# Order of VectorE's steps in the dense expert stage: subtractions behind gather steps, the steps halved and issued in quarters

## The chip, the cores and the metric

The kernel runs on one core of a Trainium2 chip. The metric is the device time of one execution in microseconds. The median of three runs of the kernel before is 2719.4 us (2717.3 to 2721.43).

## What is computed

Two transformer blocks over 512 tokens of width 1024. The change lies in the expert layer of the first, which picks 16 of 16384 experts per head and token:

```python
def peer_ffn(h, w_pq, sub_keys, expert_u, expert_v):
    ...
        q = (hb @ w_pq).reshape(TOK_BLOCK, PEER_HEADS, 2, PEER_DHALF)
        s = jnp.einsum('thpd,hpnd->thpn', q, sub_keys).astype(jnp.float32)
        ...
        top_s, pos = lax.top_k(cand_s, PEER_TOPK)
        idx = jnp.take_along_axis(cand_i, pos, axis=-1)
        gate = jax.nn.softmax(top_s, axis=-1).astype(hb.dtype)
        u = expert_u[idx]
        act = jax.nn.gelu(jnp.einsum('thkd,td->thk', u, hb), approximate=False)
        vv = expert_v[idx]
        return jnp.einsum('thk,thkd->td', gate * act, vv)
```

## The kernel before, in words

The expert layer treats the first 384 tokens and the last 128 differently. For the 384 it goes **densely** over all 16384 experts in 128 blocks of 128: up (the block's rows of `expert_u` times the tokens), gelu, times a gate that is zero where an expert was not chosen, and down (times the rows of `expert_v`), summed over all blocks in six banks. For the last 128 tokens it **gathers** the chosen rows with indirect DMAs that GpSimd issues. The dense loop is `peer_dense`, the gather `peer_gather`; a third strand, `ada`, computes the second block's modulation on VectorE. They run at the same time: `peer_dense` yields a weight, and the loop in `peer` that called it then takes as many steps of the other two as the weight is worth. All is written out when the kernel is built, so that this loop only sets the order in which each engine finds its instructions. Each engine takes them in that order.

Products are made of three matmuls with operands split in a high and a low half. ScalarE copies the high half (`whi`, `wh`, `uh`), and VectorE subtracts it from the source for the low half (`wlo`, `wl`, `ul`). In iteration i of the dense loop:

- `weigh(i - 1)` multiplies the activation with its gate on VectorE (`ga`, L1379), copies `wh` on ScalarE and returns the subtraction for `wl` (L1382) as something to be called later;
- `act(i)` is the gelu of block i out of its bank (ScalarE, L1371);
- `trans(i + 2, q)` transposes one half of a block of `expert_u` on TensorE (L1354, four transposes into the one bank `pt`), copies `uh` out of the bank and subtracts `ul` out of it (both in `split`, L86 and L87). The bank is free for the next transposes when `ul` has been read;
- `values(i - 1)` splits the rows of `expert_v` into `whi` and `wlo` (L86, L87);
- `down(i - 2, ...)` and `up(i + 1)` are the matmuls (L67 to L69), 18 with 512 columns and 24 with 384.

On TensorE an iteration is: transposes q = 0, down, transposes q = 1, up. The low halves follow their high halves at once on VectorE, but for `wl`, which is called after `trans(i + 2, 0)`. The loop yields twice per iteration, behind the first three pairs of `down` and at the end.

28 of the 128 blocks are **early**: their up and gelu were done in an earlier stage (`peer_early`), and the dense loop only loads the result. They come in groups of four between the others; an iteration of one has half the weight and neither transposes nor up.

A step of `peer_gather` for index i issues the fetch of a row of `expert_u` (`ur`) and one of `expert_v` (`vr`), two steps ahead of their use; multiplies row i of `ur` with the token's activations (L1763, the product); and adds a weighted row of `vr` to the output (L1770, the accumulation). Row buffers are four deep. A piece of the next head's selection (L1578 to L1665, a chain of short VectorE instructions) comes ahead of the product in about half of the steps. A step of `ada` is one multiply-add (L1853) on a loaded tile `aw`. There are 154 units of gather steps and 56 of `ada` steps, taken 2% ahead of the dense loop's share.

Of the kernel before, what the change touches and what calls it, by code (L numbers as in the profile page):

```python
# [10 lines left out]
F32 = mybir.dt.float32  # L11
F32R = mybir.dt.float32r
# [4 lines left out]
AF = mybir.ActivationFunctionType  # L17
ALU = mybir.AluOpType
# [4 lines left out]
D = 1024  # L23
NB = S // 128
KD = D // 128
# [30 lines left out]
class Kern:  # L56
# [1084 lines left out]
    def peer(self):  # L1141
        tc, nc, A, xt, ah, al = self.tc, self.nc, self.A, self.xt, self.ah, self.al
        v, s, pe, g = nc.vector, nc.scalar, nc.tensor, nc.gpsimd
        self.ad = self.es.enter_context(self.pool("ada"))
        self.banks = self.es.enter_context(self.pool("banks", space=PSUM))
        with self.pool("peer") as pp, self.pool("gdram", space=bass.MemoryType.DRAM) as dp:
            self.gd = dp.tile([ND // ST, NKEYS, NKEYS, ST], F32, name="gd")
            self.vb = A["expert_v"][0].rearrange("(n e) d -> n e d", e=128)
            self.ad_d = dp.tile([EARLY, 128, ND], F32, name="early")
            hT = pp.tile([128, D], F32, name="hT")  # L1150
            sc3 = pp.tile([128, 2 * HEADS, NKEYS], F32, name="sc3")
            self.lim = pp.tile([128, 2, TOPK, TOPK], F16, name="lim")
            self.num = pp.tile([128, TOPK], F16, name="num")
            for a in range(TOPK):
                for i, x in enumerate((self.START[a], a)):
                    g.memset(self.lim[:, i, a, :], float(x))
                g.memset(self.num[:, a:a + 1], float(self.CAND[a]))
            with self.pool("ptmp", side="right") as tmp:
                sel = [tmp.tile([128, NB - 1, HEADS, TOPK], F32, name=f"sel{i}") for i in range(3)]
                with self.pool("pkeys", side="right") as kp:  # L1160
                    KT = kp.tile([128, 16, 128], F32, name="KT")
                    with self.pool("pnrm", side="right") as t2:
                        self.attn_out(t2, Banks(self.banks, lin=range(4), tr=(4, 5)), hT, KT)
                    ps = Banks(self.banks, lin=(6, 7, 0, 1), sc=(2, 3), gp=(2, 3, 6, 7), eu=(4, 5))
                    self.early = self.peer_early(tmp, ps)
                    with self.pool("psel", side="right") as t2:
                        self.peer_select(t2, ps, sel, sc3, KT)
                with self.pool("pspr", side="right") as t2:
                    self.peer_spread(t2, ps, sel)
                for _ in self.early:  # L1170
                    pass
            with self.pool("pgat") as gp:
                ps = Banks(self.banks, pt=(4,), pu=(5,), **{f"pv{b}{i}": ((6, 7, 0, 1, 2, 3)[2 * b + i],) for b in range(3) for i in range(2)})
                gath = self.peer_gather(gp, NB - 1, hT, sc3)
                side = self.ada(self.ad, gp, ps)
                dense = self.peer_dense(gp, ps, itertools.chain(gath, side), hT)
                load, done = 0.0, [0, 0]
                for w in dense:
                    load += w
                    for i, (it, n) in enumerate(((gath, HEADS * TOPK + TOPK + 10), (side, 6 * (KD + 1) + 2))):  # L1180
                        while done[i] < load * n * self.HASTE:
                            next(it, None)
                            done[i] += 1
        self.show("x2", xt)
# [120 lines left out]
    def peer_dense(self, dp, ps, others, hT):  # L1305
# [35 lines left out]
                    gates[i + j] = gt[:, :, j, :]  # L1341

        def trans(i, q):
            if i >= NE or order[i] < EARLY:
                return
            if i < FIRST:
                return
            if q == 0:
                ut[i] = [dp.tile([128, KD, 128], F32R, name=nm, bufs=2) for nm in ("uh", "ul")]
            u = us[i][:, q * 512:q * 512 + 512]  # L1350
            if order[i] >= self.nt:
                p = ps.tile([128, 512], F32, name="pt")
                for j in range(4):
                    pe.transpose(p[:, j * 128:j * 128 + 128], u[:, j * 128:j * 128 + 128], self.ident)  # L1354
                u = p
            h, l = (t[:, 4 * q:4 * q + 4, :].rearrange("p k e -> p (k e)") for t in ut[i])
            self.split(h, l, u)

        def up(i):
            if i >= NE or order[i] < EARLY:  # L1360
# [22 lines left out]

        def values(i):
            if not 0 <= i < NE:
                return
            vs[i] = [self.ring.tile([128, D], F32R, name=nm, bufs=self.SPL) for nm in ("whi", "wlo")]
            self.split(*vs[i], raw.pop(i))

        def down(i, parts):  # L1390
            if i < 0:
# [14 lines left out]
        for i in range(NE):  # L1406
            load(i + 3)
            load2(i + 1)
            low = weigh(i - 1)
            act(i)  # L1410
            trans(i + 2, 0)
            low()
            values(i - 1)
            down(i - 2, pairs[:3])
            w = (0.5 if i + 1 < NE and order[i + 1] < EARLY else 1.1) / (1.1 * NE - 0.6 * EARLY)
            yield w / 2
            down(i - 2, pairs[3:])
            trans(i + 2, 1)
            up(i + 1)
            ws.pop(i - 2, None), vs.pop(i - 2, None)  # L1420
            yield w / 2
        for _ in others:
            pass
        weigh(NE - 1)()
        values(NE - 1)

        items = self.it_glu[0]
        own = [it for item in items for it, _, _ in item]
# [283 lines left out]
    def peer_gather(self, gp, b, hT, sc3):  # L1712

        nc, A, xt = self.nc, self.A, self.xt
        v, s, g = nc.vector, nc.scalar, nc.gpsimd
        U, V = A["expert_u"][0], A["expert_v"][0]
        idx, gates = {}, {}

        def select(h):
            sv, si = ([gp.tile([128, 1, TOPK], dt, name=f"{n}{c}", bufs=2) for c in range(2)]  # L1720
                      for n, dt in (("sv", F32), ("si", U32)))
            for c in range(2):
                self.top16(gp, sc3[:, 2 * h + c:2 * h + c + 1, :], sv[c], si[c])
                yield
            out = [gp.tile([128, 1, TOPK], F32, name=f"sel{i}", bufs=3) for i in range(3)]
            yield from self.pairs(gp, sv, si, out, v)
            yield
            yield from self.softmax16(gp, out[2])
            idx[h] = gp.tile([128, TOPK], I32, name="idx", bufs=3)
            v.scalar_tensor_tensor(idx[h], out[0][:, 0, :], float(NKEYS), out[1][:, 0, :], op0=ALU.mult, op1=ALU.add)  # L1730
            gates[h] = out[2][:, 0, :]
            yield

        def rows(tab, h, k, name):
            t = gp.tile([128, D], F32, name=name, bufs=4)
            g.indirect_dma_start(out=t, out_offset=None, in_=tab,  # L1736
                                 in_offset=bass.IndirectOffsetOnAxis(ap=idx[h][:, k:k + 1], axis=0))
            return t


        AHEAD, n = 2, HEADS * TOPK
        acts, ur, vr = {}, {}, {}
        sel = select(0)
        for i in range(-AHEAD, n + TOPK):
            j = i + AHEAD
            if j < n:
                if j % TOPK == 0:
                    for _ in sel:
                        if j == 0:
                            yield  # L1750
                    sel = select(j // TOPK + 1) if j + TOPK < n else iter(())
                else:
                    next(sel, None)
                ur[j] = rows(U, j // TOPK, j % TOPK, "ur")
            if TOPK <= j < n + TOPK:
                j -= TOPK
                vr[j] = rows(V, j // TOPK, j % TOPK, "vr")
            if 0 <= i < n:
                h, k = divmod(i, TOPK)
                if k == 0:  # L1760
                    acts[h] = gp.tile([128, TOPK], F32, name="act", bufs=2)
                u = ur.pop(i)
                v.scalar_tensor_tensor(u, u, 1.0, hT, op0=ALU.mult, op1=ALU.mult, accum_out=acts[h][:, k:k + 1])  # L1763
            if i >= TOPK:
                h, k = divmod(i - TOPK, TOPK)
                act = acts[h]
                if k == 0:
                    s.activation(act, act, AF.Gelu)
                    v.tensor_tensor(act, act, gates[h], op=ALU.mult)
                v.scalar_tensor_tensor(xt[:, b, :], vr.pop(i - TOPK), act[:, k:k + 1], xt[:, b, :], op0=ALU.mult, op1=ALU.add)  # L1770
            yield
# [500 lines left out]
```

## Time and profile before

| | |
|---|---|
| median of the runs | 2719.4 us |
| profiled execution | 2718.3 us, span 2716.5 us |
| busy TensorE / VectorE / ScalarE / GpSimd | 2482.5 / 1843.2 / 1009.9 / 820.2 us |
| mean granted clock of TensorE | 0.967 |
| dense stage | about 917 to 2026 us |
| 128 gate products `ga` (L1379) | 907.6 to 2016.5 us (starts) |
| 128 row products (L1763) | 982.9 to 1898.4 us (starts) |

TensorE is PE in the profile, VectorE DVE, ScalarE ACT, GpSimd POOL, SyncE SP. An idle time is put to the engine and line that ended it: "PE bank L1354 <- DVE ul L87" is TensorE, about to transpose at L1354, waiting for the `ul` subtraction. L1354 is the transposes, L67 to L69 the matmuls of both `up` and `down`. A matmul's listed duration overlaps the next one's; its pace is the distance of the starts.

### The profile page before, as it was taken

To read this page: it belongs to the slowest core of one execution; us is meant where nothing else is said; L and a number is where in the kernel's file an instruction comes from. 1 tells how busy PE (TensorE), PEld (TensorE's weight loads), DVE (VectorE), ACT (ScalarE), POOL (GpSimd) and SP (SyncE) were. 2 spreads that over 40 slices of the span, in tenths; PEclk is the share of its full clock that TensorE was granted. 3 is DMA by queue.
4 is the path that set the end of the run, shared out by engine and by line. 5 is a ranking of instruction groups with operands and counts; after the bars stand their busy time and mean duration, and the time that the engine had idled before them with its cause. 6 is when DMAs were issued, how large, how long until landed. Compare 5 with 4: busy or idle time off the path is not lost. (4 is left out here: it accounts for less than half of the span.)

```text
span 2716.5 us, 39721 instructions
## 1 busy us (share of the span) xinstructions
PE 2482.5 (91%) x15452; PEld 2076.9 (76%) x15452; DVE 1843.2 (68%) x3701; ACT 1009.9 (37%) x1589; POOL 820.2 (30%) x759
## 2 busy tenths in 40 slices
PE   7999996899788799999998999999999889899998
PEld 6775774687677789788787888889877667788887
DVE  4725654569899475877877787878666856644546
ACT  4424443433288333233232333333343224444321
POOL 3324200224500011333333333333114715433322
PEclk9999998899899899999999999999999989899999
DMA  4111246431256567888888888888742214133232
GB/s 144 43 40 55 87 170 215 159 110 62 68 224 259 207 240 258 290 295 292 297 285 284 308 296 293 308 314 301 250 136 62 78 39 142 48 96 95 93 109 77
DMA packets 222004, 484.28 MB, mean 178 GB/s; under 512 B 15560, under 2 KB 129881, under 8 KB 220280
## 3 DMA queue, kind: packets, MB, share of 16 engines
q1 hardware_dynamic: 184248, 347.29, 37.7%
q0 software_dynamic: 37568, 134.46, 13.9%
q8 instruction: 121, 1.98, 0.3%
q14 instruction: 67, 0.55, 0.1%
HBM read 432.67 MB, written 49.02 MB: 177 GB/s over the span
## 5 line engine op out<-in xcount | busy, mean ns | idle before, releaser
L1736 POOL DMA_INDIRECT ur<-in_expert_u,idx x128 | 199.3, 1557 | 776.4 <-DVE ur L1763 517.8
L86 ACT ACTIVATE whi<-raw 128x1024 fp32r<-128x1024 f32 (+1 forms) x266 | 278.4, 1047 | 410.5 <-PE bank L68 234.8
L87 DVE TENSOR_TENSOR wlo<-raw,whi 128x1024 fp32r<-128x1024 f32 (+1 forms) x199 | 250.8, 1260 | 171.0 <-ACT whi L86 167.2
L87 POOL TENSOR_TENSOR wlo<-raw,whi 128x1024 fp32r<-128x1024 f32 (+1 forms) x67 | 176.1, 2628 | 562.8 <-ACT whi L86 540.8
L67 PE MATMUL bank<-whi,wh 128*128 128x512 f32 x768 | 313.5, 408 | 2.6 <-ACT whi L86 2.5
L68 PE MATMUL bank<-wlo,wh 128*128 128x512 f32 x768 | 306.3, 399 | 2.8 <-DVE wlo L87 2.8
L69 PE MATMUL bank<-whi,wl 128*128 128x512 f32 x768 | 306.3, 399 | 0.0
L69 PE MATMUL bank<-ah,wlo 128*128 128x512 f32 (+2 forms) x688 | 272.4, 396 | 14.6 <-POOL wlo L87 10.8
L67 PE MATMUL bank<-ah,uh 128*128 128x384 f32 (+1 forms) x816 | 281.7, 345 | 2.5 <-ACT ga L1371 2.5
L67 PE MATMUL bank<-ah,whi 128*128 128x512 f32 (+2 forms) x688 | 274.4, 399 | 1.5 <-ACT ah L1527 0.9
L68 PE MATMUL bank<-al,uh 128*128 128x384 f32 (+1 forms) x816 | 273.6, 335 | 1.4 <-POOL al L1822 1.3
L69 PE MATMUL bank<-ah,ul 128*128 128x384 f32 (+1 forms) x816 | 273.2, 335 | 0.0
L68 PE MATMUL bank<-al,whi 128*128 128x512 f32 (+2 forms) x688 | 272.0, 395 | 0.0
L87 DVE TENSOR_TENSOR ul<-bank,uh 128x512 fp32r<-128x512 f32 x194 | 133.8, 690 | 201.8 <-ACT uh L86 201.8
L1381 ACT ACTIVATE wh<-ga 128x384 fp32r<-128x384 f32 x128 | 67.2, 525 | 532.6 <-DVE ga L1379 491.9
L86 ACT ACTIVATE uh<-bank 128x512 fp32r<-128x512 f32 x194 | 115.2, 594 | 171.2 <-PE bank L1354 171.2
L1736 POOL DMA_INDIRECT vr<-in_expert_v,idx x128 | 136.7, 1068 | 125.3 <-DVE xt L1770 91.1
L68 PEld LDWEIGHTS bank<-wlo,wh 128*128 128x128 f32 x768 | 145.9, 190 | 35.8 <-DVE wlo L87 4.7
L67 PEld LDWEIGHTS bank<-whi,wh 128*128 128x128 f32 x768 | 146.0, 190 | 34.2 <-ACT whi L86 3.7
L69 PEld LDWEIGHTS bank<-whi,wl 128*128 128x128 f32 x768 | 145.5, 189 | 34.5
L1354 PE MATMUL bank<-ident,ub 128*128 128x128 f32 x776 | 120.8, 279 | 55.7 <-DVE ul L87 45.2
L69 PEld LDWEIGHTS bank<-ah,wlo 128*128 128x128 f32 x688 | 132.1, 192 | 47.1 <-POOL wlo L87 13.0
(585 smaller groups left out, 5673.6 us busy)
## 6 DMA issues: line engine op xcount, KB each, us to landing
raw<-in_expert_v SPq DMA_DIRECT2D x128, 512.0 KB, 5.2
ub<-in_expert_u SPq DMA_DIRECT2D x97, 512.0 KB, 4.4
raw<-in_w_in SPq DMA_DIRECT2D x48, 512.0 KB, 3.8
gd<-gst SPq DMA_DIRECT2D x12, 2048.0 KB, 7.1
gb<-gd SPq DMA_DIRECT2D x32, 768.0 KB, 8.0
aw<-in_w_ada SPq DMA_DIRECT2D x48, 512.0 KB, 7.9
raw<-in_w_up SPq DMA_DIRECT2D x44, 512.0 KB, 3.6
utd<-wlo SPq DMA_DIRECT2D x31, 512.0 KB, 3.0
```

The costliest lines, as they stand in the source:

```text
L67: mm(ps, lh, rh, start=first, stop=False)
L68: mm(ps, lh, rl, start=False, stop=False)
L69: mm(ps, ll, rh, start=False, stop=last)
L86: self.nc.scalar.activation(hi, src, AF.Copy)
L87: (eng or self.nc.vector).tensor_tensor(lo, src, hi.bitcast(F32), op=ALU.subtract)
L1354: pe.transpose(p[:, j * 128:j * 128 + 128], u[:, j * 128:j * 128 + 128], self.ident)
L1381: s.activation(wh, a, AF.Copy)
L1736: g.indirect_dma_start(out=t, out_offset=None, in_=tab, in_offset=bass.IndirectOffsetOnAxis(ap=idx[h][:, k:k + 1], axis=0))
```

## The change

The subtractions of `trans` and `values` are no longer issued with their high halves. Both functions now return them, as `weigh` did, and the loop calls them behind a yield. It yields four times per iteration, a quarter of the weight each. A gather step is divided in two by a yield between the product and the accumulation, and its number of units goes from 154 to 300. In an iteration VectorE so gets: `ga`; first portion of the other strands; `wl`, `ul` of q = 0; second portion; `wlo`; third portion; `ul` of q = 1; fourth portion.

```diff
-                    for i, (it, n) in enumerate(((gath, HEADS * TOPK + TOPK + 10), (side, 6 * (KD + 1) + 2))):
+                    for i, (it, n) in enumerate(((gath, 2 * (HEADS * TOPK + TOPK) + 12), (side, 6 * (KD + 1) + 2))):
...
         def trans(i, q):
-            if i >= NE or order[i] < EARLY:
-                return
-            if i < FIRST:
-                return
+            if i >= NE or order[i] < EARLY or i < FIRST:
+                return lambda: None
...
-            self.split(h, l, u)
+            s.activation(h, u, AF.Copy)
+            return lambda: v.tensor_tensor(l, u, h.bitcast(F32), op=ALU.subtract)
...
         def values(i):
             if not 0 <= i < NE:
-                return
-            vs[i] = [self.ring.tile([128, D], F32R, name=nm, bufs=self.SPL) for nm in ("whi", "wlo")]
-            self.split(*vs[i], raw.pop(i))
+                return lambda: None
+            vh, vl = vs[i] = [self.ring.tile([128, D], F32R, name=nm, bufs=self.SPL) for nm in ("whi", "wlo")]
+            x = raw.pop(i)
+            s.activation(vh, x, AF.Copy)
+            return lambda: v.tensor_tensor(vl, x, vh.bitcast(F32), op=ALU.subtract)
...
             load(i + 3)
             load2(i + 1)
-            low = weigh(i - 1)
+            w = (0.5 if i + 1 < NE and order[i + 1] < EARLY else 1.1) / (1.1 * NE - 0.6 * EARLY)
+
+            wl = weigh(i - 1)
             act(i)
-            trans(i + 2, 0)
-            low()
-            values(i - 1)
+            ul = trans(i + 2, 0)
+            yield w / 4
+            wl()
+            ul()
+            vl = values(i - 1)
             down(i - 2, pairs[:3])
-            w = (0.5 if i + 1 < NE and order[i + 1] < EARLY else 1.1) / (1.1 * NE - 0.6 * EARLY)
-            yield w / 2
+            yield w / 4
+            vl()
             down(i - 2, pairs[3:])
-            trans(i + 2, 1)
+            ul = trans(i + 2, 1)
+            yield w / 4
+            ul()
             up(i + 1)
             ws.pop(i - 2, None), vs.pop(i - 2, None)
-            yield w / 2
+            yield w / 4
...
-        values(NE - 1)
+        values(NE - 1)()
...
                 v.scalar_tensor_tensor(u, u, 1.0, hT, op0=ALU.mult, op1=ALU.mult, accum_out=acts[h][:, k:k + 1])
+            yield
             if i >= TOPK:
```

The first place is VectorE in the middle of the stage, at the second selection chain of a head (MAX to MAX_INDEX). Here `ur,act<-ur,hT` is the product, `xt<-vr,act,xt` the accumulation, `aacc` a modulation step, `ul<-bank` the low half of a transposed block. Before:

```order
L87 TENSOR_TENSOR ul<-bank_12175,uh 128x512
L1578 MAX sv_12151<-sc_5078 128x8
L1580 MAX_INDEX si_12153<-sv_12151,sc_5078 128x8
L1583 MATCH_REPLACE scr_12207<-sv_12151,sc_5078 128x128
L1578 MAX sv_12151<-scr_12207 128x8
L1580 MAX_INDEX si_12153<-sv_12151,scr_12207 128x8
L1763 SCALAR_TENSOR_TENSOR ur,act<-ur,hT 128x1024
L1769 TENSOR_TENSOR act<-act,sel_10253 128x16
L1770 SCALAR_TENSOR_TENSOR xt<-vr,act,xt 128x1024
L1853 SCALAR_TENSOR_TENSOR aacc<-aw,silc,aacc 128x1024
L1379 TENSOR_TENSOR ga<-ga,gb 128x384
L87 TENSOR_TENSOR ul<-bank_12237,uh 128x512
```

And now, at the same selection chain of that head, with the line numbers of the changed kernel:

```order
L1378 TENSOR_TENSOR ga<-ga,gb 128x384
L1585 MAX sv_11923<-sc_5078 128x8
L1587 MAX_INDEX si_11925<-sv_11923,sc_5078 128x8
L1590 MATCH_REPLACE scr_11998<-sv_11923,sc_5078 128x128
L1585 MAX sv_11923<-scr_11998 128x8
L1587 MAX_INDEX si_11925<-sv_11923,scr_11998 128x8
L1770 SCALAR_TENSOR_TENSOR ur,act<-ur,hT 128x1024
L1381 TENSOR_TENSOR wl<-ga,wh 128x384
L1356 TENSOR_TENSOR ul<-bank_11992,uh 128x512
L1777 TENSOR_TENSOR act<-act,sel_9969 128x16
L1778 SCALAR_TENSOR_TENSOR xt<-vr,act,xt 128x1024
L1389 TENSOR_TENSOR wlo<-raw,whi 128x1024
```

The selection and the product stood ahead of `ga` and stand behind it, between `ga` and its block's `ul`; the accumulation has gone behind that `ul`.

The second place is VectorE at the start of the stage, where `ul<-ub` are the halves of the one block that is read already transposed. Before:

```order
L87 TENSOR_TENSOR ul<-ub,uh 128x512
L1578 MAX sv_9471<-sc_5078 128x8
L1580 MAX_INDEX si_9473<-sv_9471,sc_5078 128x8
L1583 MATCH_REPLACE scr_9475<-sv_9471,sc_5078 128x128
L1578 MAX sv_9471<-scr_9475 128x8
L1580 MAX_INDEX si_9473<-sv_9471,scr_9475 128x8
L1851 TENSOR_SCALAR aacc<-aw,silc 128x1024
L87 TENSOR_TENSOR ul<-ub,uh 128x512
```

And now:

```order
L1585 MAX sv_9470<-sc_5078 128x8
L1587 MAX_INDEX si_9472<-sv_9470,sc_5078 128x8
L1590 MATCH_REPLACE scr_9474<-sv_9470,sc_5078 128x128
L1585 MAX sv_9470<-scr_9474 128x8
L1587 MAX_INDEX si_9472<-sv_9470,scr_9474 128x8
L1859 TENSOR_SCALAR aacc<-aw,silc 128x1024
L1356 TENSOR_TENSOR ul<-ub,uh 128x512
```

The first `ul` has gone behind the first modulation step.

## Rows read from the trace of the kernel before

**Rows 1.** Stretches of the dense stage: length; busy per engine (instructions); granted clock; DMA share, GB/s.

```profile
1090.00:1280.00 190.00, 176.36 (x900) 154.28 (x898) 151.51 (x297) 58.55 (x95) 67.09 (x50) 0.97 0.84 292
1280.00:1460.00 180.00, 168.36 (x872) 146.07 (x872) 142.87 (x265) 57.39 (x95) 67.82 (x50) 1.00 0.84 297
1460.00:1640.00 180.00, 167.41 (x867) 146.12 (x866) 145.22 (x274) 57.24 (x93) 66.19 (x49) 0.98 0.84 293
1640.00:1780.00 140.00, 132.21 (x676) 114.32 (x675) 112.96 (x200) 44.30 (x72) 52.26 (x39) 0.99 0.86 305
...
sum 1109.00, PE 1058.02 PEld 926.05 DVE 830.90 ACT 362.87 POOL 335.97; mean PE 132.25 PEld 115.76 DVE 103.86 ACT 45.36 POOL 42.00
```

**Rows 2.** TensorE's waits, 917 to 2026: waiter <- releaser: total us, times, longest.

```profile
PE bank L1354 <- DVE ul L87: 39.3, 36, 2.5
PE bank L68 <- DVE wlo L87: 2.8, 4, 0.8
PE bank L67 <- ACT whi L86: 2.5, 2, 1.6
PE bank L67 <- ACT ga L1371: 2.5, 2, 2.0
```

**Rows 3.** VectorE's waits, 1090 to 1780.

```profile
DVE ul L87 <- ACT uh L86: 102.1, 67, 2.9
DVE wl L1382 <- ACT wh L1381: 10.5, 16, 0.7
DVE wlo L87 <- ACT whi L86: 9.9, 16, 1.4
```

**Rows 4.** VectorE: start us, us, engine, line, operation [idle before <- releaser].

```profile
1206.63 0.28 DVE L1578 MAX8 sv<-sc 128x8 f32<-128x128 f32 x1
...
1208.21 1.21 DVE L1763 SCALAR_TENSOR_TENSOR ur<-ur,hT 128x1024 f32<-128x1024 f32 x1
...
1209.55 1.28 DVE L1770 SCALAR_TENSOR_TENSOR xt<-vr,act,xt 128x1024 f32<-128x1024 f32 x1
1210.75 1.28 DVE L1853 SCALAR_TENSOR_TENSOR aacc<-aw,silc,aacc 128x1024 f32<-128x1024 f32 x1
1211.95 0.60 DVE L1379 TENSOR_TENSOR ga<-ga,gb 128x384 f32<-128x384 f32 x1
1214.06 0.69 DVE L87 TENSOR_TENSOR ul<-bank,uh 128x512 fp32r<-128x512 f32 x1 [1.51 <-ACT uh L86]
...
1997.34 0.69 DVE L87 TENSOR_TENSOR ul<-bank,uh 128x512 fp32r<-128x512 f32 x1 [3.36 <-ACT uh L86]
```

**Rows 5.** ScalarE in the same block.

```profile
1213.43 0.59 ACT L86 ACTIVATE uh<-bank 128x512 fp32r<-128x512 f32 x1
```

**Rows 6.** TensorE in the same block.

```profile
1207.47 0.60 PE L1354 MATMUL bank<-ident,ub 128*128 128x128 f32 x4
...
1214.80 1.11 PE L1354 MATMUL bank<-ident,ub 128*128 128x128 f32 x4 [2.53 <-DVE ul L87]
```

**Rows 7.** TensorE's transposes in a block without a stall.

```profile
1882.60 0.60 PE L1354 MATMUL bank<-ident,ub 128*128 128x128 f32 x4
...
1887.23 0.60 PE L1354 MATMUL bank<-ident,ub 128*128 128x128 f32 x4
...
1891.84 0.60 PE L1354 MATMUL bank<-ident,ub 128*128 128x128 f32 x4
```

**Rows 8.** Transposes back to back, the first and the last of seven.

```profile
981.46 0.66 PE L1354 MATMUL bank<-ident,ub 128*128 128x128 f32 x4 [1.41 <-DVE ul L87]
...
1975.77 0.66 PE L1354 MATMUL bank<-ident,ub 128*128 128x128 f32 x4 [1.41 <-DVE ul L87]
```

**Rows 9.** A stretch behind the stall at 1214.80, columns as in rows 1.

```profile
1214.80:1218.10 3.30, 3.30 (x12) 3.30 (x13) 3.07 (x13) 0.77 (x2) 0.00 (x0) 0.50 0.63 195
```

**Rows 10.** VectorE at the start of the stage.

```profile
904.80 0.76 DVE L1851 TENSOR_SCALAR aacc<-aw,silc 128x1024 f32<-128x1024 f32 x1 [4.39 <-DMA aw<-in_w_ada]
...
909.69 0.69 DVE L87 TENSOR_TENSOR ul<-bank,uh 128x512 fp32r<-128x512 f32 x1 [1.50 <-ACT uh L86]
```

## The prediction

> **What bounds the kernel now.** I read the page first: TensorE is busy for 91% of the span and its granted clock is mostly full, so only stages in which TensorE waits can give anything. The change touches one stage, the dense one, 917 to 2026 us in the trace. The table of stretches comes next [rows 1]: over those 1109 us TensorE is busy 1058.0, so 51.0 us are idle, and nearly all of that lies in 1090 to 1780, where the four stretches have 176.4 + 168.4 + 167.4 + 132.2 = 644.3 busy of 690, 45.7 idle. The deficit of the granted clock there, 190 x 0.03 + 180 x 0.02 + 140 x 0.01, is another 10.7 us. At full pace these 690 us would thus take about 634.
>
> TensorE's waits say who is late [rows 2]: 39.3 of the 51.0 us end with VectorE's `ul`, the low half of a transposed expert block, which must be read out of the one bank for transposes before the next transposes may write there. Some 7.8 us end with `wlo`, `whi` or the gelu `ga`, in the groups of four early blocks.
>
> VectorE's own waits show why it is late although it is busy only 552.6 of those 690 us (the sum of its column in [rows 1]): 102.1 us waiting in front of `ul` for ScalarE's `uh` [rows 3]. One block shows the chain [rows 4 to 6]. TensorE transposes at 1207.47 and then has other matmuls, until 1214.80 - 2.53 = 1212.27. VectorE meanwhile works through a selection (1206.63 to 1208.21), a row product, an accumulation and a modulation step, and comes to `ga` only at 1211.95. Its end at 1212.55 releases ScalarE's `wh`, gelu, `uh` (1213.43), and VectorE, with `ul` next in its queue, stands still for 1.51 us. `ul` ends at 1214.75, TensorE resumes at 1214.80 after 2.53 us. A `ul` right behind a `ga` occurs 97 times in the stage, and VectorE waits before every one, 1.50 us at the first [rows 10] and 3.36 at the last, at 1997.34 [rows 4], 1.5 in the median: time per block in which gather work could have run. A block without a stall takes 1891.84 - 1882.60 = 9.24 us on TensorE [rows 7].
>
> **The change part by part.** No instruction is added or taken away; TensorE, SyncE and GpSimd keep their orders (of ScalarE's, only the gathers' exponents and gelus move a little). What moves is VectorE's order.
>
> *The first portion now stands between `ga` and `ul`, `wl` ahead of `ul`.* Where the portion holds a product or an accumulation (1.2 us from start to next start, 1209.55 to 1210.75 in [rows 4]), the chain `wh`, gelu, `uh` runs under it and the 1.51 us go to nothing. Where it is empty, `wl` (about 0.5) comes once `wh` is there and some 1.0 us of waiting stays. In the new order 38 of 97 blocks with `ul` have it empty: 0.39 x 1.0 = 0.4 us a block instead of 1.5.
>
> Is that enough? Per block VectorE's steps from start to next start are about 3.3 us of dense work; a block carries 1.36 gather steps of 2.35 us = 3.2 (1.02 x 300 half steps x 1.1 / 124 a block, from the code, halved), half a modulation step 0.6 (1210.75 to 1211.95 is one) and, in the half of the time when a selection runs, one of its pieces a step, up to 1.6 us (1206.63 to 1208.21), some 1.2 on average: 1.36 x 1.2 = 1.6 us more. That makes 8.7 us in selection stretches, 7.1 outside. With 1.5 us of waiting a selection block needs 10.2 us against TensorE's 9.24: VectorE is the bound there, and the stalls come in those runs. With 0.4 it needs 9.1, about even; outside 7.5. So the stalls on `ul` should mostly go. As a check by sums: 552.6 busy + about 21 (54 blocks x 0.4) + some 35 for the other waits is 609, under the 634 that TensorE needs.
>
> *What stays of the 39.3.* Seven of these stalls come where two transposes stand back to back, because the block between is early and has no up matmuls; the first and the last took 1.41 [rows 8], the seven together 11.1 us. No order of VectorE's queue takes the chain uh, ul away there. So 28.2 us are open. I walked one selection through the new order from block to block with these durations: `ga` then ends between 2.0 us before and 1.1 us after the start of the transposes, and the first `ul` ends 0.3 to 2.7 us before the next transposes want the bank. The margin is thin at one end, so I leave 4 to 5 us of stall: **-24 us** (bounds -12, if half stays, and -28).
>
> *The early groups.* There VectorE waited for `wh` and `whi` too, 10.5 and 9.9 us [rows 3]; portions now stand in front of `wl` and `wlo`. Of TensorE's 7.8 us I take **-3** (0 to -7.8).
>
> *The clock.* After the stall of 2.53 us the granted clock is 0.50 for 3.3 us [rows 9], the lower of its two levels, 1.2 GHz for 2.4, and half of that time is lost. Of the 10.7 us of deficit above, the windows that follow ordinary stalls should go, others follow early groups and back-to-back transposes: **-4** (-1.7 to -8).
>
> *The start.* VectorE's first modulation step waits 4.39 us for its DMA, until 904.80 [rows 10]. One `ul` and a part of the first selection that stood before it or behind `ga` now stand between it and the first `ga`, some 0.6 + 0.7 us, and the first portion has about 1 us of selection. TensorE already waits there until 910.44 for that `ul`. **+1.5** (+1 to +3, as the clock is low there). Back-to-back transposes: one of the seven has a portion of some 2.8 us ahead of its `ul`; it mostly runs under the transposes, **+0.5** (0 to +3).
>
> SyncE's loads and GpSimd's fetches keep their place. The accumulation of a step comes half a step later than now, by some 3.4 us, which delays the release of one of four row buffers; VectorE's waits name no fetched row [rows 3], so I cost that at nothing. If that cover were gone, the product would wait in front of `ul`.
>
> Sum: -24 - 3 - 4 + 1.5 + 0.5 = -29 us. The profiled execution took 2718.3 us (span 2716.5), 1.1 under the median of the runs, 2719.4. The forecast against the median is 2719.4 - 29 = **2690**.
>
> **One bank for the transposes: a rule against this change.** In the rows the bank is free in time wherever VectorE is: 1887.23 - 1882.60 = 4.63 us lie from transpose to transpose [rows 7], and where nothing lies between them the chain holds TensorE for 1.41 [rows 8]. The Trainium skill (Perfetto Trace Analysis, section Matmuls) says that independent matmul groups should rotate through different PSUM banks, so that emptying one overlaps the next group; this kernel gives the transposes a single one. By that rule alone the bank is the cause, no new order on VectorE helps, and nothing is gained. The trace bears it out for the seven back-to-back cases only.
>
> **The rivals.**
> *Half stays.* VectorE remains the bound in selections, since 9.1 us a block is as much as TensorE's 9.24, and a portion with a selection and a product delays the block after it. For it: the thin margins. Against: the lighter stretches between. Then -12 - 1.5 - 2 + 2 = -13.5: 2706.
>
> *Slower: the portion ahead of `ul` is itself the wait.* In 17 of the 97 blocks the first portion is a selection piece with a product, or a product with an accumulation, 2.4 to 3.0 us. With `wl` (0.47) and `ul` (0.61) behind it, the bank is free 3.5 to 4.1 us after `ga`'s end, against 2.1 now. The limit is some 4.55 us after the start of the transposes [rows 7]. It decides where `ga` ends later than 0.4 us after that start: in the block of [rows 4, 6] `ga` ended at 1212.55, 5.1 us after it. If VectorE stays as late as it is now, each of the 17 pays 2.0 us, +33, against which the gain of 24 and the start's +1.5 leave about +10: 2730. Against it: with the lumps quartered, the portion before `ga` is shorter by as much.
>
> *Nothing:* the idle time goes over to another releaser (the bank as by the rule above, the gelu's bank, the fetches): 2718, within 0.2%.
>
> **How the numbers follow.** Forecast 0.66, half stays 0.18, nothing 0.07, slower 0.09. My own terms at their better ends give -28 - 7.8 - 8 + 1 = -43, 2676, which is the low end; at their worse ends -12 - 0 - 1.7 + 6 = -8, 2711, the high end, which takes in the half case. Beyond 2711 lie most of "nothing" and "slower", 0.16. About 0.2%, 5 us, is what a measurement of this kernel can tell from no change: faster 0.85, the same 0.06, slower 0.09.
>
> **What would show it.** Right: TensorE's wait for `ul` in the dense stage falls from 39.3 to about 16 us, 11 of it at the back-to-back transposes; VectorE's wait before `ul` falls to less than half; VectorE's busy time stays the same in a stage that is about 29 us shorter; the clock's deficit in 1090 to 1780 is about 6. Wrong: the wait for `ul` stays at 30 or more, with a product or a selection directly ahead of those `ul` (slower), or VectorE idles little and TensorE still waits (half), or TensorE's waits turn to `wlo`, the gelu or the bank of the gelu (nothing).

## The result and the profile after

The changed kernel takes 2687.43 us in the median of four runs (2683.09 to 2688.15); the kernel before, over four runs, 2720.15. The ratio is 0.9878, with a 95% interval of 0.9865 to 0.9891: 32.7 us faster, where the forecast was 29 us and 2690. In a later series on one chip both kernels ran once more: 2722.53 and 2682.96 us, 39.6 us faster, 0.9852 (0.9832 to 0.9873).

The dense stage of the profiled execution, cut into stretches (columns as in [rows 1]):

```profile
1100.00:1280.00 180.00, 178.32 (x944) 158.84 (x943) 151.48 (x269) 62.48 (x101) 64.92 (x52) 1.00 0.90 322
1280.00:1455.00 175.00, 169.60 (x879) 148.96 (x878) 147.16 (x296) 57.62 (x95) 59.80 (x48) 0.99 0.85 301
1455.00:1630.00 175.00, 171.89 (x906) 151.66 (x905) 144.74 (x247) 61.34 (x98) 59.70 (x50) 1.00 0.89 319
1630.00:1760.00 130.00, 125.54 (x656) 111.42 (x655) 108.33 (x195) 43.76 (x71) 44.05 (x36) 0.99 0.87 308
...
sum 1068.50, PE 1046.31 PEld 924.52 DVE 828.94 ACT 366.99 POOL 311.93; mean PE 130.79 PEld 115.57 DVE 103.62 ACT 45.87 POOL 38.99
```

Against [rows 1] the stage lasts 1068.5 us instead of 1109.0. VectorE is busy for the same time (828.9 and 830.9), so nothing was saved there; TensorE's idle time fell from 51.0 to 22.2 us. TensorE's waits in the stage, which answer to [rows 2]:

```profile
PE bank L1352 <- DVE ul L1356: 14.7, 9, 3.7
PE bank L68 <- DVE wlo L1389: 4.4, 5, 2.1
```

The wait for `ul` fell from 39.3 to 14.7 us and from 36 times to 9; the waits for `whi` and for the gelu are gone; that for `wlo` grew by 1.6. VectorE's own wait for `uh`, over the stretch that answers to [rows 3] (1097 to 1749):

```profile
DVE ul L1356 <- ACT uh L1355: 43.8, 48, 1.8
DVE wl L1381 <- ACT wh L1380: 20.0, 31, 0.7
DVE wlo L1389 <- ACT whi L1388: 18.2, 24, 3.1
```

The wait before `ul` was 102.1, 67 times. Those before `wl` and `wlo` grew from 20.4 to 38.2 us, so that of the 122.5 us of the three rows 82.0 are left. One block shows how `ul` gained. VectorE:

```profile
1209.92 0.55 DVE L1378 TENSOR_TENSOR ga<-ga,gb 128x384 f32<-128x384 f32 x1
...
1212.22 1.22 DVE L1770 SCALAR_TENSOR_TENSOR ur<-ur,hT 128x1024 f32<-128x1024 f32 x1
...
1213.36 0.55 DVE L1381 TENSOR_TENSOR wl<-ga,wh 128x384 fp32r<-128x384 f32 x1
1213.83 0.68 DVE L1356 TENSOR_TENSOR ul<-bank,uh 128x512 fp32r<-128x512 f32 x1
1214.43 1.28 DVE L1778 SCALAR_TENSOR_TENSOR xt<-vr,act,xt 128x1024 f32<-128x1024 f32 x1
```

ScalarE and TensorE in the same block:

```profile
1210.57 0.53 ACT L1380 ACTIVATE wh<-ga 128x384 fp32r<-128x384 f32 x1 [3.89 <-DVE ga L1378]
1211.00 0.47 ACT L1370 ACTIVATE ga<-bank 128x384 f32<-128x384 f32 x1
1211.37 0.59 ACT L1355 ACTIVATE uh<-bank 128x512 fp32r<-128x512 f32 x1
```

```profile
1210.05 0.60 PE L1352 MATMUL bank<-ident,ub 128*128 128x128 f32 x4
...
1214.68 0.60 PE L1352 MATMUL bank<-ident,ub 128*128 128x128 f32 x4
```

The same three steps of ScalarE still stand between `ga` and `ul`, but a selection piece and a product now run under them, so that neither `wl` nor `ul` shows an idle time. `ul` ends at 1214.51, the transposes start at 1214.68, 4.63 us after the last ones, with no wait: the pace of [rows 7].

### The profile page after: what moved, and what is told of

It reads as the page before. It is cut to its first block, busy times and chain, and to the rows that moved or that the text cites. A ratio compares the mean times of both kernels' runs of the same rounds, so it can differ in the third digit from the quotient of the medians.

```text
span 2686.4 us, 39748 instructions
## 1 busy us (share of the span) xinstructions
PE 2479.2 (92%) x15452; PEld 2080.9 (77%) x15452; DVE 1848.4 (69%) x3701; ACT 1013.9 (38%) x1589; POOL 795.5 (30%) x759
## 5 line engine op out<-in xcount | busy, mean ns | idle before, releaser
L1743 POOL DMA_INDIRECT ur<-in_expert_u,idx x128 | 156.5, 1223 | 579.8 <-DVE ur L1770 385.8
L86 ACT ACTIVATE whi<-raw 128x1024 fp32r<-128x1024 f32 (+1 forms) x138 | 143.3, 1039 | 412.3 <-PE bank L68 235.5
L69 PE MATMUL bank<-ah,wlo 128*128 128x512 f32 (+2 forms) x688 | 272.8, 397 | 14.6 <-POOL wlo L87 10.8
L1743 POOL DMA_INDIRECT vr<-in_expert_v,idx x128 | 155.4, 1214 | 301.5 <-DVE xt L1778 299.6
L87 DVE TENSOR_TENSOR wlo<-raw,whi 128x1024 fp32r<-128x1024 f32 (+1 forms) x71 | 94.5, 1331 | 138.3 <-ACT whi L86 138.2
L1389 DVE TENSOR_TENSOR wlo<-raw,whi 128x1024 fp32r<-128x1024 f32 x128 | 156.4, 1222 | 44.7 <-ACT whi L1388 44.0
L67 PEld LDWEIGHTS bank<-whi,wh 128*128 128x128 f32 x768 | 145.6, 190 | 30.5 <-ACT whi L1388 0.3
```

Of the source, the lines that this page charges most:

```text
L67: mm(ps, lh, rh, start=first, stop=False)
L69: mm(ps, ll, rh, start=False, stop=last)
L86: self.nc.scalar.activation(hi, src, AF.Copy)
L87: (eng or self.nc.vector).tensor_tensor(lo, src, hi.bitcast(F32), op=ALU.subtract)
L1389: return lambda: v.tensor_tensor(vl, x, vh.bitcast(F32), op=ALU.subtract)
L1743: g.indirect_dma_start(out=t, out_offset=None, in_=tab, in_offset=bass.IndirectOffsetOnAxis(ap=idx[h][:, k:k + 1], axis=0))
```

## The experiments

The table holds, for each kernel's profile, what I worked out from the positions of its TensorE instructions: the start of the stage's first transposes, from there to the first `down` matmul ("start"), from there to the transposes that follow the stage ("dense"), and in "dense" TensorE's idle time, the part of it that ends with `ul`, and half of the time at the lower of the clock's two levels.

| kernel | first transposes at | start | dense | idle | of it `ul` | clock |
|---|---|---|---|---|---|---|
| before | 903.4 | 13.8 | 1109.0 | 51.0 | 39.6 | 10.2 |
| after | 910.7 | 16.1 | 1068.5 | 22.2 | 14.8 | 5.1 |
| after, again | 906.5 | 16.1 | 1068.5 | 22.2 | 14.8 | 5.1 |
| e1_no_defer | 903.2 | 14.0 | 1103.6 | 43.1 | 34.2 | 13.7 |
| e2_whole_steps | 909.3 | 14.9 | 1094.4 | 38.7 | 26.2 | 10.2 |
| e3_first_portion_only | 905.7 | 14.3 | 1108.4 | 49.1 | 38.7 | 15.4 |
| e4_ul_first | 912.3 | 14.0 | 1101.2 | 43.7 | 33.8 | 8.5 |
| e5_apart | 902.9 | 14.6 | 1064.3 | 16.8 | 9.3 | 6.8 |
| e6_aw_first | 908.4 | 9.8 | 1071.5 | 22.2 | 14.8 | 8.5 |
| e7_both | 904.9 | 9.8 | 1066.0 | 16.8 | 9.2 | 8.5 |
| e7_again | 902.9 | 10.8 | 1063.3 | 17.0 | 9.6 | 5.1 |
| e8_uh_first | 910.7 | 12.5 | 1130.7 | 63.7 | 41.5 | 17.1 |
| e9_both_uh_first | 910.5 | 7.0 | 1058.4 | 13.0 | 5.6 | 5.1 |

**One half of the change at a time.** My theory was that the chain `ga`, `wh`, gelu, `uh`, `ul`, which stood uncovered on VectorE's queue, was the loss (theory A). The rival: the gather work came in two lumps per block, and smaller lumps alone do it (theory B). e1 keeps the smaller lumps and takes the deferral back, against the changed kernel:

```diff
-            ul = trans(i + 2, 0)
-            yield w / 4
+            trans(i + 2, 0)()
             wl()
-            ul()
-            vl = values(i - 1)
+            values(i - 1)()
+            yield w / 4
             down(i - 2, pairs[:3])
             yield w / 4
-            vl()
             down(i - 2, pairs[3:])
-            ul = trans(i + 2, 1)
+            trans(i + 2, 1)()
             yield w / 4
-            ul()
```

> The changed kernel with every subtraction issued at once again (ul right behind its uh, wl and wlo ahead of the first portion); four portions and halved steps stay. Theory A (what counts is that the first portion runs under the chain wh, gelu, uh behind ga): VectorE waits some 1.5 us before the ul behind every ga again, the wait of TensorE for ul in the dense stage stays near 30 to 40 us, 2710 to 2718 us. Theory B (what counts is that the lumps of gather work ahead of ga are smaller): most of the gain stays, TensorE's wait for ul under 20 us, 2690 to 2698 us.

Measured 2715.5 us, ratio 0.9983 (0.9973 to 0.9992): 5 of the 33 us. VectorE's wait over the stage (925 to 2010; 202.6 us in the kernel before, from 917 to 2026) is what it was:

```profile
DVE ul L1356 <- ACT uh L1355: 197.1, 127, 3.5
```

With the subtractions back at once, smaller lumps alone do not do it: B falls. e4 leaves all of the change but puts `ul` and `wl` ahead of the first portion again:

```diff
-            yield w / 4
-            wl()
             ul()
+            wl()
+            yield w / 4
             vl = values(i - 1)
```

> The changed kernel with the first ul and wl ahead of the first portion (ul right behind ga); wlo and the second ul stay deferred, four portions, halved steps. Theory A: the wait of 1.5 us before the ul behind ga is back in every block, and with it TensorE's wait for ul, 25 to 40 us: 2708 to 2718 us. Theory B: 2688 to 2695 us, as changed.

Measured 2717.05 us, 0.9981 (0.9971 to 0.9992). Without the first portion between `ga` and `ul`, nearly the whole gain is gone, and VectorE's wait is back (925 to 2010):

```profile
DVE ul L1356 <- ACT uh L1355: 195.9, 114, 3.5
```

e3 does that part alone. It starts from the kernel before, with its whole steps and two portions, and has the first portion ahead of `wl` and `ul` (beside the same changes to `trans` and `values`):

```diff
-            low = weigh(i - 1)
-            act(i)
-            trans(i + 2, 0)
-            low()
-            values(i - 1)
-            down(i - 2, pairs[:3])
...
+            wl = weigh(i - 1)
+            act(i)
+            ul = trans(i + 2, 0)
             yield w / 2
+            wl()
+            ul()
+            values(i - 1)()
+            down(i - 2, pairs[:3])
             down(i - 2, pairs[3:])
-            trans(i + 2, 1)
+            trans(i + 2, 1)()
```

> The kernel before with one thing moved: its first of two portions now stands between ga and wl, ul (wlo and the second ul at once, whole steps). Theory A: the smallest edit that covers the chain, so more than half of the gain: 2695 to 2705 us, VectorE's wait before ul at half of before; some lumps of 4 to 5 us ahead of ul cost TensorE 10 to 20 us. Theory B: no smaller lumps, so nothing gained: 2714 to 2725 us.

Measured 2721.29 us, 1.000 (0.9989 to 1.0012): nothing, where I had expected more than half of the gain from A. VectorE's wait before the first `ul` of a block did fall, from 166 to 31 us (worked out over the 97 blocks), and that before the second rose from 36 to 123. But 17 of TensorE's 24 stalls on `ul`, 28.6 of 38.5 us, now come before the transposes that need the first `ul` (20 of 36, 19.7 of 39.3 us, in the kernel before). Two blocks of it on VectorE show the price, the lump at full size:

```profile
1201.18 0.55 DVE L1378 TENSOR_TENSOR ga<-ga,gb 128x384 f32<-128x384 f32 x1
...
1205.56 0.55 DVE L1381 TENSOR_TENSOR wl<-ga,wh 128x384 fp32r<-128x384 f32 x1
1206.03 0.68 DVE L1356 TENSOR_TENSOR ul<-bank,uh 128x512 fp32r<-128x512 f32 x1
...
1208.09 0.69 DVE L1356 TENSOR_TENSOR ul<-bank,uh 128x512 fp32r<-128x512 f32 x1 [0.25 <-ACT uh L1355]
...
1214.01 0.59 DVE L1378 TENSOR_TENSOR ga<-ga,gb 128x384 f32<-128x384 f32 x1
```

and TensorE:

```profile
1206.77 0.66 PE L1352 MATMUL bank<-ident,ub 128*128 128x128 f32 x4 [0.40 <-DVE ul L1356]
...
1216.87 0.66 PE L1352 MATMUL bank<-ident,ub 128*128 128x128 f32 x4 [0.62 <-DVE ul L1356]
```

Between `ga` and `wl` lie 3.9 us of selection, product and accumulation instead of 1.5 us of waiting, and between the second `ul` and the next `ga` another 5.2. Both lumps lead to a stall of TensorE. So A alone falls too: in this form, with whole steps and only two portions, covering the chain gains nothing. e2 keeps the four portions and the deferral but leaves the gather step whole (without its `yield`, 154 units again):

```diff
-enumerate(((gath, 2 * (HEADS * TOPK + TOPK) + 12), (side, 6 * (KD + 1) + 2))):
+enumerate(((gath, HEADS * TOPK + TOPK + 10), (side, 6 * (KD + 1) + 2))):
```

> The changed kernel with whole gather steps (no yield between product and accumulation, 154 units); deferred subtractions and four portions stay. Theory A: the chain is still covered wherever the first portion has a step, but in fewer blocks, and lumps of 2.4 to 4 us stand ahead of some ul: 2692 to 2702 us, TensorE's wait for ul 20 to 30 us. Theory B: the gain goes for the most part, 2708 to 2718 us.

Measured 2708.85 us, 0.9953 (0.9937 to 0.9968), the range that I had given for B. The waits (TensorE 915 to 2030, VectorE 925 to 2010):

```profile
PE bank L1352 <- DVE ul L1356: 32.7, 25, 6.5
PE bank L68 <- DVE wlo L1389: 8.2, 8, 2.5
DVE wl L1381 <- ACT wh L1380: 62.8, 92, 1.4
```

The longest of the first row is the start; 26.2 us in 24 stalls lie in the dense stage. VectorE waits as little before the first `ul` as in the changed kernel (48.5 us, 49.0 there), but more before `wl` (62.8 us, 40.3 there): 65 of the 97 first portions are empty instead of 38. Yet before 18 of the 24 stalls VectorE did not wait for `uh`: `ul` stood behind work, mostly a whole step, and ran late. The halved step is worth the difference, 26 of the 40.5 us of the dense stage, by both effects together. How the other 14 us, from e3 to e2, divide between the four portions and the two further subtractions that e2 puts off was not tried apart.

**The largest rests of the changed kernel.** Seven pairs of transposes stand back to back, and the start of the stage waits on a modulation step. e5 moves the second transposes of an iteration ahead of the last three of its six pairs of `down` where no `up` follows:

```diff
+            apart = i + 1 < NE and order[i + 1] < EARLY
+            if apart:
+                ul = trans(i + 2, 1)
             down(i - 2, pairs[3:])
-            ul = trans(i + 2, 1)
+            if not apart:
+                ul = trans(i + 2, 1)
```

e6 has the modulation strand load its first tile before the dense loop begins (a `yield` behind its `load(0)`, and this line):

```diff
                 side = self.ada(self.ad, gp, ps)
+                next(side)
```

e7 does both; the changed kernel ran with them once more.

> The changed kernel once more, as the base of this series and for the part of the time that lies ahead of the dense stage. If the 7 us by which its first dense transposes came later than in the kernel before (910.7 against 903.4 us) are drift from run to run, they come at another time here, between 903 and 912; if the edit causes them, at 910 to 911 again. The time 2684 to 2690 us either way.

> The changed kernel with one reordering on TensorE: in the seven iterations in which no up follows, the second transposes come between the third and fourth pair of down matmuls instead of behind the last, so that no two transposes stand back to back. If the stalls there (13.0 us in the changed kernel) are the bare chain uh, ul behind a single bank, 2.1 us of matmuls on either side cover most of them: 8 to 12 us less than the changed kernel, TensorE's wait for ul 2 to 6 us. If VectorE is late there anyway, the stalls only move: within 3 us of the changed kernel.

> The changed kernel with the first load of the modulation weights issued ahead of the dense stage's first loads. If VectorE's wait for that load is what makes the first ga late, TensorE's stall of 7.2 us at the start falls to 2 to 4 and the kernel gains 3 to 5 us; if the block of expert_u that TensorE waits for only lands later by as much, nothing changes (within 1 us).

> The two edits before together: the sum of what each gives, 11 to 17 us less than the changed kernel, if the two stalls are independent; about 2671 to 2677 us.

On one chip: after again 2682.96 us (1 us under the range that I had given; its first transposes came at 906.5, so that their time drifts from run to run), e5 2679.49, e6 2678.8, e7 2673.95. e5's dense stage is 4.2 us shorter, less than I expected: three pairs of `down` between the two transposes, 2.1 us, are too little where VectorE comes late. TensorE in e5:

```profile
1628.53 0.66 PE L1352 MATMUL bank<-ident,ub 128*128 128x128 f32 x4 [1.44 <-DVE ul L1356]
...
1633.32 0.65 PE L1352 MATMUL bank<-ident,ub 128*128 128x128 f32 x4 [2.04 <-DVE ul L1356]
```

e6's start fell from 16.1 to 9.8 us, and TensorE's stall in it from 7.2 to 1.7, where I had expected 2 to 4; its dense stage has the same idle time as the changed kernel's and 3.4 us more of low clock, which took half of that back. e7 has the gains of both in its idle times and no more: I had expected 11 to 17 us and got 9.0.

**The chain itself.** If the place of `uh` behind `ga`, `wh` and gelu is the loss, `uh` can simply go first. e8 does that in the kernel before, by issuing the transposes and their split ahead of `weigh` and `act`:

```diff
+            trans(i + 2, 0)
             low = weigh(i - 1)
             act(i)
-            trans(i + 2, 0)
             low()
```

> The kernel before with one reordering: the transposes and the copy uh of the next block are issued ahead of ga, wh and the gelu, so that on ScalarE uh no longer stands behind wh, and on VectorE ul stands ahead of ga. Theory A in its narrow form (ul is late because uh queues behind wh on ScalarE, and wh waits for ga): TensorE's wait for ul falls to the back-to-back cases, 12 to 20 us, 2690 to 2702 us. Against it: VectorE's idle time only moves to wl and wlo, which now wait for wh and whi behind ga (0.6 + 0.9 us a block, as much as the 1.5 us at ul), so that VectorE stays as late as it was and the time falls little, 2708 to 2718 us.

Measured 2745.93 us, 1.0078 (1.0054 to 1.0103): slower, against both expectations. ScalarE in e8, VectorE, and TensorE:

```profile
1218.05 0.60 ACT L86 ACTIVATE uh<-bank 128x512 fp32r<-128x512 f32 x1 [2.36 <-PE bank L1354]
1223.72 0.52 ACT L1381 ACTIVATE wh<-ga 128x384 fp32r<-128x384 f32 x1 [5.07 <-DVE ga L1379]
1224.15 0.47 ACT L1371 ACTIVATE ga<-bank 128x384 f32<-128x384 f32 x1
```

```profile
1222.48 0.68 DVE L87 TENSOR_TENSOR ul<-bank,uh 128x512 fp32r<-128x512 f32 x1
1223.08 0.55 DVE L1379 TENSOR_TENSOR ga<-ga,gb 128x384 f32<-128x384 f32 x1
1224.27 0.56 DVE L1382 TENSOR_TENSOR wl<-ga,wh 128x384 fp32r<-128x384 f32 x1 [0.65 <-ACT wh L1381]
1225.60 1.23 DVE L87 TENSOR_TENSOR wlo<-raw,whi 128x1024 fp32r<-128x1024 f32 x1 [0.77 <-ACT whi L86]
```

```profile
1223.21 0.66 PE L1354 MATMUL bank<-ident,ub 128*128 128x128 f32 x4 [1.05 <-DVE ul L87]
1224.67 0.44 PE L67 MATMUL bank<-ah,uh 128*128 128x384 f32 x1 [0.80 <-ACT ga L1371]
```

`uh` is early, at 1218.05, but its `ul` still stands behind a lump and comes 3.8 us later. The bubble went to the next links: `wl` waits 0.65 for `wh`, `wlo` 0.77 for `whi`, and the gelu, now behind the late `ga`, holds its bank so that `up` waits too (13.8 us in all, 14 times). Of the 21.7 us by which the dense stage grew, 12.7 are idle time and 6.9 low clock. With the lumps large and nothing between a high half and its low half, this order only trades one wait for another.

e9 puts `uh` first on ScalarE in e7, that is with the small portions and the deferral, and `ul` ahead of `wl`:

```diff
+            ul = trans(i + 2, 0)
             wl = weigh(i - 1)
             act(i)
-            ul = trans(i + 2, 0)
             yield w / 4
-            wl()
             ul()
+            wl()
```

> The changed kernel with the separated transposes and the early modulation load once more, as the base for the run before: 2670 to 2677 us.

> The changed kernel with the separated transposes and the early modulation load, and with uh ahead of wh on ScalarE and ul ahead of wl. If what is left of the wait for ul (9 us) comes from blocks in which ga is late, it falls to 3 or less and the time by 4 to 8 us against the kernel with the two edits; if VectorE itself is late there, nothing (within 2 us).

On one chip e9 took 2670.44 us (0.9807 of the kernel before, 0.9782 to 0.9832), e7 2678.94 (0.9841), 2 us above the range that I had given. The gain of 8.5 us is a little over my 4 to 8, but the single runs overlap (2666.3 to 2673.35 and 2671.31 to 2681.61); in the profiles e9's dense stage and start are 4.9 and 3.8 us shorter than those of that second profile of e7, at the same 5.1 us of low clock. TensorE's wait in e9 (925 to 1985), where I had expected 3 us or less:

```profile
PE bank L1353 <- DVE ul L1357: 5.3, 4, 2.8
```

It is the fastest of the kernels here, 54 us under the kernel before on that chip (2724.1). There e8 was 22 us slower than the kernel before: the move that costs there gains some 5 us of the stage once the chain is covered.

## Why the prediction was right, step by step

**The stalls on `ul`, -24.** The ordinary ones went from 28.2 to 1.6 us, -26.6. The chain was the cause, as e1 and e4 show by leaving it uncovered, with the lumps around it as the second half of the cause. But the prediction named the cover and took the small lumps as its condition only in passing (the margin "from 2.0 us before to 1.1 after"); e2 and e3 show that the lumps decide whether the cover pays. The walk through one selection held for most blocks: `ga` now ends, relative to the transposes' start, at a median of +0.16 us (it was +1.14), with -2.18 and +0.93 at the first and the eighth tenth; in 18 of the 97 it is later than the +1.1 of the walk (49 before). The count of empty portions held, 38 of 97, but not their price: VectorE waits 1.45 us before their `wl` and `ul` together, not 1.0, and in 20 blocks with a portion something is left as well. Over all blocks that is 0.77 us a block (74 us) instead of 0.4. TensorE's ordinary stalls fell all the same. VectorE's wait for `uh` in the stretch of [rows 3] fell to 43%, but over both `ul` of the 97 blocks only from 202 to 116 us: before the second `ul` it rose from 36 to 67, which costs nothing: both ordinary stalls that are left end with a first `ul`.

**The back-to-back transposes, +0.5.** Measured +1.9 (11.1 to 13.0), all of it at one with a portion ahead of its `ul`, as named (1.55 to 3.70). TensorE, then VectorE:

```profile
1640.26 0.60 PE L1352 MATMUL bank<-ident,ub 128*128 128x128 f32 x4
1644.56 0.66 PE L1352 MATMUL bank<-ident,ub 128*128 128x128 f32 x4 [3.70 <-DVE ul L1356]
```

```profile
1639.97 1.23 DVE L1389 TENSOR_TENSOR wlo<-raw,whi 128x1024 fp32r<-128x1024 f32 x1 [0.25 <-ACT whi L1388]
1641.11 0.29 DVE L1585 MAX8 sv<-sc 128x8 f32<-128x128 f32 x1
...
1642.69 1.21 DVE L1770 SCALAR_TENSOR_TENSOR ur<-ur,hT 128x1024 f32<-128x1024 f32 x1
...
1643.82 0.69 DVE L1356 TENSOR_TENSOR ul<-bank,uh 128x512 fp32r<-128x512 f32 x1
```

I had the portion "mostly run under the transposes"; it starts 0.85 us after the start of the first transposes and ends 3.6 after it, because `wlo`, late in a group of early blocks, stands ahead of it. The bounds (0 to +3) held it.

**The early groups, -3.** 7.8 to 4.4, -3.4, with the releaser changed: `whi` and gelu gone, `wlo` up. **The clock, -4.** The deficit of the dense stage went from 10.2 (10.7 in the prediction, from rounded rows) to 5.1, -5.1. The two profiles of e7 differ by 3.4 in it, so that this match may be luck in part. **The start, +1.5.** 13.8 to 16.1, +2.3: the wait for `ul` there rose from 5.88 to 7.22, by the 1.3 I had summed up, and the rest went at the lower clock. The wait for the modulation tile is not longer: the step begins 1.4 us after the first transposes in both kernels (912.07 against 910.7, 904.80 against 903.4), and its row below lists more idle time only because the `ul` that stood ahead of it now stands behind. What grew is the work between the step and `ga`. e6 shows that most of the stall hangs on that step: without the wait for the tile it is 1.7 us. In the changed kernel VectorE stands before it; in e6 the step finds its tile there:

```profile
912.07 0.75 DVE L1859 TENSOR_SCALAR aacc<-aw,silc 128x1024 f32<-128x1024 f32 x1 [17.24 <-DMA aw<-in_w_ada]
```

```profile
902.75 0.75 DVE L1861 TENSOR_SCALAR aacc<-aw,silc 128x1024 f32<-128x1024 f32 x1
```

**The sum.** My terms for the dense stage were -24, -3, -4 and +0.5, -30.5; it became 40.5 us shorter. The rows give 28.8 of idle time and 5.1 of clock; nearly all of the rest is a term that I had not got at all (last section). The whole execution became 30.1 us shorter in the profiles (2716.5 to 2686.4), because the first transposes came 7.3 us later in this profile and the start took 2.3 more. That the forecast of 29 is so near to the 32.7 of the medians is thus partly luck: the stage gave 10 us more than forecast, and some of it is hidden by what happened ahead of the stage. In the later series, where the first transposes came at 906.5, the gain was 39.6.

**The rivals.** *Half stays* did not come: e2 is that case, with 26.2 us of `ul` left, 2708.85. *Slower* has its mechanism in e3: a portion ahead of `ul` that is itself the wait. There it took back the whole gain, and no more. In the changed kernel 13 first portions are longer than 2.4 us (I had counted 17), and in only 4 of these does `ga` end more than 0.4 us after the transposes' start, from which I had let it decide; the latest, at 1.14, costs TensorE 0.12 us. In e3 they are 24 of the 50 portions from 2.3 us on. *Nothing* did not come: with the one bank kept, the ordinary stalls fell to 1.6 us, so the bank alone did not make them. The rule of the Trainium skill (Perfetto Trace Analysis, section Matmuls) that independent matmul groups should rotate through different PSUM banks does bear on the back-to-back transposes, which are 13.0 of the 14.8 us that remain. e5 spread these and got 5.5 us. A second bank was not tried; it might have taken away the ordinary stalls too.

## What to carry to other kernels

An engine that is 80% busy can still be the bound, where it stands still a fixed time in every block before an instruction whose operand another engine is still making: look for one wait of the same size that repeats, and put independent work between the producer and the consumer in the queue. That work has to be in small pieces: here the cover with whole steps gave nothing with two portions (e3) and 12 us with four (e2), small pieces without the cover 5 us, both together 33 to 40. Moving the producer forward instead cost 22 us on its own (e8), since it moved the wait to the next links, and gained only after that.

## What was not expected of the hardware

**A stall costs more than the idle time that the profile lists.** Matmuls with 512 columns start every 0.23 us, but each is listed with 0.40. The last ones ahead of the stall of [rows 6], on TensorE of the kernel before:

```profile
1211.64 0.39 PE L68 MATMUL bank<-wlo,wh 128*128 128x512 f32 x1
1211.88 0.40 PE L69 MATMUL bank<-whi,wl 128*128 128x512 f32 x1
```

The next instruction would have been due at 1211.88 + 0.23 = 1212.11, and came at 1214.80: 2.69 us lost, of which the idle time lists 2.53. My sum lacked this. Taken over all idle times of the dense stage, from the start of the matmul before to the start of the one after, less the median pace of its shape, TensorE lost 61.0 us at 56 places where 51.0 are listed in the kernel before, and 26.7 at 23 where 22.2 are listed in the changed one. The part that no wait shows so fell from 10.0 to 4.5 us, 5.5 of the 6.6 left over above.

**The time ahead of the stage differs more from execution to execution than the stage itself.** Two profiles of the changed kernel have the first transposes at 910.7 and 906.5 us and a dense stage of 1068.5 in both, at the same low clock; the two of e7 have 1066.0 and 1063.3, with 8.5 and 5.1 us of low clock. Over all kernels the first transposes lie between 902.9 and 912.3, with the same instructions of TensorE ahead of them. The stretches from 0 to 300 and 300 to 600 us, in the changed kernel and then in e5, columns as in [rows 1]:

```profile
0.00:300.00 300.00, 273.54 (x2975) 199.68 (x2977) 153.26 (x340) 125.68 (x199) 100.60 (x133) 0.98 0.25 75
300.00:600.00 300.00, 261.84 (x2378) 209.26 (x2375) 149.39 (x422) 121.68 (x254) 36.19 (x79) 0.91 0.43 148
```

```profile
0.00:300.00 300.00, 274.72 (x3073) 202.35 (x3075) 157.70 (x346) 126.94 (x201) 101.97 (x134) 0.99 0.24 76
300.00:600.00 300.00, 261.35 (x2316) 209.38 (x2313) 151.94 (x436) 123.13 (x255) 38.28 (x80) 0.93 0.43 148
```

The granted clock is a little lower in the changed kernel in both. By the trace's own records, the clock is at its lower level for 13.7 us in the first stretch against 6.8 in e5, and for 51.2 against 44.4 in the second; half of the differences is 6.8 of the 7.8 us between their first transposes. What makes the clock fall more often in one execution than in another stays open. So a change of one stage is better read from that stage's own length, beside its time at the lower clock, than from the median of a few runs.
